# Moving half of a late adaLN into the first stage, and splitting the GDN preparation into a key and a query part

## The chip, the core and the metric

The kernel runs on one core of one Trainium2 chip. TensorE (PE) multiplies matrices, VectorE (DVE), ScalarE (ACT) and GpSimd (POOL) do the element-wise work, and SyncE (SP) and ScalarE issue the DMAs. The metric is the device time of one execution in microseconds; a time is the median of several runs.

## The reference

One layer of a hybrid diffusion backbone over 1024 latent tokens and 256 context tokens, 1024 features wide, float32. Cut to what matters here:

```python
sh1, sc1, g1, sh2, sc2, g2 = split(silu(c) @ ada_w + ada_b, 6)      # adaLN
h = modulate(rms_norm([ctx; x]), sh1, sc1)                          # context has its own sh, sc
p = h @ w_in                                                        # q k v | z | a b | rq rk rv rg
q, k, v = silu(short_conv(...))                                     # 5 taps along the tokens, per segment
# gated delta rule (GDN), chunks of 64, forward and backward:
A = strict_lower(kb @ k.T * decay); u, w = solve(I + A, [v*beta, kb*exp(G)])
# scan over chunks with qk = q @ k.T * decay; retention scan over rq, rk, rv
x = x + g1 * (concat(o_gdn, o_ret) @ w_out)
x = x + g2 * swiglu(modulate(rms_norm(x), sh2, sc2))
out = rms_norm(x)
```

The first two of the six adaLN vectors (sh1, sc1) are needed at once, the other four (g1, sh2, sc2, g2; the "late adaLN") only after the scans.

## The kernel before, in words

Tokens are cut into ten tiles of 128 (two of context, 0 and 1, and eight latent, 2 to 9). Float32 products are made of three matmuls of split operands: `split` (L343) has ScalarE copy a high part (`whi`, `hhi`) and VectorE or GpSimd subtract it to get the low part (`wlo`, `hlo`).

The program is staged as follows. Names are those that the profile prints.

1. First stage. `normalize` (L317) and `modulate` (L306) make the normalized, modulated and turned tokens `hhi`/`hlo`, in four groups of tiles (`XGROUPS`: [2,3], [4,5], [6,7,8,9], [0,1]). Token groups 0 and 1, projections with tokens as rows (matmuls `tm`, L371 to L373; 24 matmuls per tile and group of 256 columns), run while the next group is normalized.
2. `ada_rest(c, half)` (L488), the late adaLN: eight units. A unit loads 2 MB of weights in four DMAs on SP (tile `adaw2`, two buffers), adds them up on VectorE in eight operations (`acc`, L497 and L499), sums over partitions on TensorE (`gr`) and stores a row or adds a bias (L505, L512). Before, units (2,0) and (2,1) stand behind the first stage, (3,0), (3,1), (4,0), (4,1) in the loop over the k convolutions, and (5,0), (5,1) in the loop over the q convolutions.
3. Token groups 2 to 5, the small decay quantities (L563 to L598), then the k convolutions: `conv_block` (L601) of heads 4 to 7. A block is three column blocks (256 of context, 512, 512) of 24 matmuls, copied by ScalarE into `u` and, scaled, into `y` (L614, L615); VectorE adds the other four taps to `y` (L621), and ScalarE applies silu (L624). `kstat` (L634) transposes k (`kt`), makes norms and stores. A store of y goes to DRAM.
4. The q convolutions (heads 0 to 3, without context), then token groups 6 and 7 (the retention gate: ScalarE's Silu from `tm` into `res`, L532; stored as `rd`).
5. `solve(0)` and `solve(1)`. Tiles are in three batches: BATCH = [[0,1,2,9],[3,8,4,7],[5,6]]. For every tile of the batch `pre(t)` (L700) loads keys `kc` and queries `qc`, multiplies k with k (`kk`), transposes q (`qt`) for its norms (ScalarE squares, L712), and multiplies k with q (`kq`). For each of two directions it loads a broadcast row `gw`, has GpSimd select its triangle (`e`, L722), ScalarE take its exponential (L726; the table of Exp), and VectorE multiply it with `kk` (`ut`, L730, stored as `un`) and with `kq` (`sp`, L732); ScalarE and GpSimd make the other half of `sp` (L735, L736), stored in `sd`. `invert(b)` (L743) then reads `un` back (`yr`) and inverts triangular blocks on VectorE in 31 steps of two operations (`tmp` L765, `X` L767).
6. The v convolutions (heads 8 to 11), each followed by transposes on TensorE (`vT`, L856), scaled copies on ScalarE (`vt`, L859) and a store. Then `pre` of the third batch, the `merge` of the inverses (`m`), `invert(2)`, token groups 8 and 9 (z), and the scans, output projection and FFN.

The order of each engine's instructions is fixed when the kernel is built: the framework simulates a timeline and picks, among what is ready, what comes first in the program. Every engine then executes its list strictly in that order. So the v convolutions are interleaved with token groups and with `pre` and `invert`, though the program has them one after the other. PSUM banks for short products (`kk`, `qt`, `kq`, `gr`, `kt`) come from one group (`bank_b`), those of `tm` and of convolutions from two others. A pool's tiles are taken over by a later pool only when all uses are over; the memory for a stage is that of a pool opened and closed around it: `W2` and `R2` live from the first stage to the end of token group 7, then `GU`, `GI` and `GP`.

Of the kernel before, what the change touches and what calls it, by code (L numbers as in the profile page):

```python
# [38 lines left out]
def build(nc, tc, ap, dbg=None, stop=None, marks=None):  # L39
# [151 lines left out]
    try:  # L191
# [264 lines left out]
        for t in (6, 7, 8, 9, 0, 1):  # L456
            load_x(t)
        hold = None
# [3 lines left out]
        for gi, grp in enumerate(XGROUPS):  # L462
# [14 lines left out]
            if gi + 2 < len(XGROUPS):  # L477
                normalize(gi + 2, hold)
        close(P0)
# [3 lines left out]
        R2 = pool("r2", bufs=2)  # L483
        ada2 = C.tile([P, 2, KT], F32, tag="ada2", name="ada2")
        grow = [dr.tile([1, D], F32, tag="grow%d" % i, name="grow%d" % i) for i in range(2)]

        def ada_rest(c, half):

            c0 = c * D + half * 512
            src = ap["ada2"][2 * (c - 2) + half]  # L490
            acc = R2.tile([P, 512], F32, tag="acc", name="acc", bufs=1)
            for k in range(KT):
                if k % 2 == 0:
                    w = R2.tile([P, 2, 512], F32, tag="adaw2", name="adaw2", bufs=2)
                    SY.dma_start(w, src[k // 2])
                if k == 0:
                    V.tensor_scalar(acc, w[:, 0], csl[:, k, 0:1], None, ALU.mult)  # L497
                else:
                    V.scalar_tensor_tensor(acc, w[:, k % 2], csl[:, k, 0:1], acc, ALU.mult, ALU.add)  # L499
            ps = bank_b("gr")  # L500
            if c in (2, 5):
                row = R2.tile([1, 512], F32, tag="row", name="row", bufs=1)
                SY.dma_start(row, ap["adarow"][c0:c0 + 512].unsqueeze(0))
                T.matmul(ps[:1, :], ones[:, 0:1], acc, start=True, stop=True)
                V.tensor_tensor(row, row, ps[:1, :], ALU.add)  # L505
                SY.dma_start(grow[0 if c == 2 else 1][:, half * 512:(half + 1) * 512], row)
            else:
                for k in range(4):
                    T.matmul(ps[:, 2 * k:2 * k + 2], acc[:, k * P:(k + 1) * P], ones[:, 0:2], start=True, stop=True)
                ks = slice(half * 4, half * 4 + 4)  # L510
                o = ada2[:, c - 3, ks]
                V.tensor_tensor(o, ps[:, 0:8].rearrange("p (k t) -> p k t", t=2)[:, :, 0],  # L512
                                adab[:, 8 * c + 4 * half:8 * c + 4 * half + 4], ALU.add)
                if c == 4:
                    V.scalar_tensor_tensor(o, o, 1.0, gffn[:, ks], ALU.add, ALU.mult)

        nA = R2.tile([P, 8], F32, tag="nA", name="nA", bufs=1)

# [16 lines left out]
        for g in range(2):  # L535
            ada_rest(2, g)
        checkpoint("rv")

# [26 lines left out]
        V.tensor_scalar(av3[:, 1], xa[:, :, 8:16], -1.0, None, ALU.mult)  # L565
        S.activation(nA, small["alog"], AF.Exp)
# [9 lines left out]
        S.activation(be, xa[:, :, 8:16], AF.Exp, scale=-1.0)  # L576
        V.tensor_scalar(sm["beta"], sm["beta"], 1.0, None, ALU.add)
# [99 lines left out]
        for h in range(H):  # L677
            y = newy()
# [976 lines left out]
```

## Time and profile before

| | us |
|---|---|
| median of 3 runs | 1481.49 |
| the runs' range | 1479.01 to 1481.59 |
| the profiled execution | 1477.96 |
| its span | 1476.2 |
| TensorE busy | 1397.2 |
| VectorE busy | 964.6 |
| ScalarE busy | 614.0 |
| GpSimd busy | 590.3 |

The profile is of one execution. Its span is from the first to the last instruction; 1.8 us of the execution's time lie around it. An operation is named by its line and by "output<-inputs"; "xN" counts instructions. A float32 product on 128 columns counts as two matmuls in the trace where the program's order has one. A row "A <- B: total, times, longest" says that A's engine stood idle for that time until B was done. Times are in us from the start of the span, single durations in us in timelines and in ns in groups.

### The profile page before, as it was taken

The numbers are of one execution on the slowest core, as the hardware profiler recorded it, in microseconds if no ns is written. First come the engines' busy times: TensorE is split into PE (matmuls) and PEld (weight loads), VectorE is DVE, ScalarE is ACT, GpSimd is POOL, SyncE is SP. The second block draws the span as 40 slices with busy tenths as digits, with TensorE's granted clock in tenths as the row PEclk, the third lists the DMA queues.
The fourth block names the chain that finished last, engine by engine and source line by source line (L and its number), as shares of the span: only waits on it lengthen the run. The fifth ranks groups of instructions, "written<-read, shape, count | busy, mean of one in ns | idle before, by whom it ended". The sixth has DMA issues, their size and how long they took to land.

```text
span 1476.2 us, 24111 instructions
## 1 busy us (share of the span) xinstructions
PE 1397.2 (95%) x8919; PEld 1199.2 (81%) x8919; DVE 964.6 (65%) x1856; ACT 614.0 (42%) x1326; POOL 590.3 (40%) x501
## 2 busy tenths in 40 slices
PE   7999999986789999899799899999999999999997
PEld 2898888975689999898688688877888888788885
DVE  6566789289792435689676877556555564657477
ACT  5643564587333111245443623233333332444445
POOL 0120010243202344234144688898555552335321
PEclk9999999998899999999899999999999999999999
DMA  9536686688888625996532265674222242776863
GB/s 337 197 105 205 189 249 200 219 264 277 282 216 277 238 76 178 416 341 209 184 125 104 97 238 210 242 264 162 105 97 105 107 151 79 260 260 194 288 216 114
DMA packets 170421, 298.14 MB, mean 202 GB/s; under 512 B 43496, under 2 KB 93880, under 8 KB 165952
## 3 DMA queue, kind: packets, MB, share of 16 engines
q1 hardware_dynamic: 118752, 253.17, 50.2%
q10 hardware_dynamic: 49072, 35.83, 7.8%
q0 software_dynamic: 2480, 7.60, 1.4%
q8 instruction: 70, 1.15, 0.3%
q14 instruction: 47, 0.39, 0.1%
HBM read 206.60 MB, written 89.96 MB: 201 GB/s over the span
## 4 chain that ended last, share of the span: by engine, by line
PE 55%; POOL 6%; DMA 5%; DVE 4%; issue 2%; ACT 2%; SPq 1%; ACTq 0%; POOLq 0%; DVEq 0%
PE ffn L1344 7%; PE ffn L1342 6%; PE ffn L1343 6%; PE fo L1470 4%; PE fo L1469 4%; PE fo L1468 4%; PE tm L371 3%; PE tm L373 3%; PE tm L372 3%; PE op L1203 2%; PE op L1201 2%; PE op L1202 2%; DMA wd<-tw 2%; POOL ws L1315 1%; DMA pk<-sd 1%
## 5 line engine op out<-in xcount | busy, mean ns | idle before, releaser
L371 PE MATMUL tm<-whi,hhi 128*128 128x256 f32 (+1 forms) x704 | 199.5, 287 | 7.7 <-ACT vt L859 3.4
L372 PE MATMUL tm<-wlo,hhi 128*128 128x256 f32 (+1 forms) x704 | 199.3, 285 | 2.4 <-issue 2.0
L373 PE MATMUL tm<-whi,hlo 128*128 128x256 f32 (+1 forms) x704 | 197.7, 285 | 0.0
L371 PEld LDWEIGHTS tm<-whi,hhi 128*128 128x128 f32 x704 | 132.8, 190 | 11.8 <-ACT vt L859 3.6
L1342 PE MATMUL ffn<-t,whi 128*128 128x512 f32 x352 | 136.9, 390 | 1.3 <-ACT whi L344 1.3
L1344 PE MATMUL ffn<-t,wlo 128*128 128x512 f32 x352 | 137.0, 390 | 1.0 <-DVE wlo L345 1.0
L1343 PE MATMUL ffn<-t,whi 128*128 128x512 f32 x352 | 137.0, 389 | 0.0
L372 PEld LDWEIGHTS tm<-wlo,hhi 128*128 128x128 f32 x704 | 133.7, 190 | 2.1 <-issue 0.9
L373 PEld LDWEIGHTS tm<-whi,hlo 128*128 128x128 f32 x704 | 132.8, 190 | 2.6 <-issue 1.8
L344 ACT ACTIVATE whi<-wraw 128x512 fp32r<-128x512 f32 (+2 forms) x98 | 75.1, 771 | 141.4 <-PE ffn L1343 80.5
L344 ACT ACTIVATE whi<-ws 128x512 fp32r<-128x512 f32 x88 | 55.6, 632 | 171.5 <-PE ffn L1343 123.4
L345 DVE TENSOR_TENSOR wlo<-ws,whi 128x512 fp32r<-128x512 f32 x88 | 93.9, 1068 | 47.0 <-ACT whi L344 46.8
L1469 PE MATMUL fo<-wlo,ahi 128*128 128x512 f32 x308 | 120.2, 390 | 2.1 <-DVE wlo L345 2.1
L1468 PE MATMUL fo<-whi,ahi 128*128 128x512 f32 x308 | 119.3, 390 | 0.7 <-ACT ahi L344 0.7
L1470 PE MATMUL fo<-whi,alo 128*128 128x512 f32 x308 | 119.0, 390 | 0.0
L345 DVE TENSOR_TENSOR wlo<-wraw,whi 128x512 fp32r<-128x512 f32 (+2 forms) x92 | 99.4, 1082 | 24.6 <-ACT whi L344 24.6
L1342 PE MATMUL ffn<-b,whi 128*128 128x512 f32 x264 | 103.8, 393 | 4.4 <-ACT whi L344 4.4
L1344 PE MATMUL ffn<-b,wlo 128*128 128x512 f32 x264 | 103.6, 393 | 0.8 <-DVE wlo L345 0.8
L1343 PE MATMUL ffn<-b,whi 128*128 128x512 f32 x264 | 103.4, 392 | 0.0
L612 PE MATMUL b<-hlo,whi 128*128 128x512 f32 (+1 forms) x256 | 94.4, 369 | 0.0
L613 PE MATMUL b<-hhi,wlo 128*128 128x512 f32 (+1 forms) x256 | 94.3, 368 | 0.0
L611 PE MATMUL b<-hhi,whi 128*128 128x512 f32 (+1 forms) x256 | 94.3, 368 | 0.0
(446 smaller groups left out, 3448.1 us busy)
## 6 DMA issues: line engine op xcount, KB each, us to landing
adaw<-ada SPq DMA_DIRECT2D x48, 512.0 KB, 4.4
pk<-sd SPq DMA_DIRECT2D x16, 1536.0 KB, 10.0
wraw<-wfi SPq DMA_DIRECT2D x44, 512.0 KB, 3.7
ar<-ad SPq DMA_DIRECT2D x33, 512.0 KB, 4.7
w<-wfo SPq DMA_DIRECT2D x22, 512.0 KB, 5.7
wd<-tw SPq DMA_DIRECT2D x11, 1024.0 KB, 4.8
ad<-act SPq DMA_DIRECT2D x20, 512.0 KB, 3.0
raw<-wd SPq DMA_DIRECT2D x20, 512.0 KB, 4.9
```

Of the source, the lines that this page charges most:

```text
L344: S.activation(hi, raw, AF.Copy)
L345: e.tensor_tensor(lo, raw, hi.bitcast(F32), ALU.subtract)
L371: T.matmul(o, hhi[:, k, tsl], whi[:, k % 4, :], start=(k == 0), stop=False)
L372: T.matmul(o, hhi[:, k, tsl], wlo[:, k % 4, :], start=False, stop=False)
L373: T.matmul(o, hlo[:, k, tsl], whi[:, k % 4, :], start=False, stop=(k == KT - 1))
L612: T.matmul(o, whi[:, k, :], hl, start=False, stop=False)
L1342: T.matmul(o, whi[:, k, :], xhi(xn, slice(0, 4), k), start=(first and k == 0), stop=False, **kw)
L1343: T.matmul(o, whi[:, k, :], xlo(xn, slice(0, 4), k), start=False, stop=False, **kw)
L1344: T.matmul(o, wlo[:, k, :], xhi(xn, slice(0, 4), k), start=False, stop=(k == 3), **kw)
L1468: T.matmul(po[g][i], ahi[:, ts], whi, start=(j == 0 and not kw), stop=False, **kw)
L1469: T.matmul(po[g][i], ahi[:, ts], wlo, start=False, stop=False, **kw)
L1470: T.matmul(po[g][i], alo[:, ts], whi, start=False, stop=(j == FH - 1), **kw)
```

## The change

- `ada_rest` is defined earlier and takes a pool, tags and a number of buffers. Units (2,0), (2,1), (3,0), (3,1) come one each behind the four groups of the first stage, with memory from a new pool `R3`. Units (4,0), (4,1), (5,0), (5,1) come in the loop over the q convolutions, with memory from `GP`, under tags that `pre` uses as well. The loop over the k convolutions has none any more.
- `W2` is closed before the small decay quantities and `R2` opened after them and closed behind the k convolutions; `GU`, `GI` and `GP` open there. Token groups 6 and 7 take their weights from `W`, loaded on ScalarE's queue instead of SP's.
- `pre` has a key part (`kk`, `ut`, the store of `un`) and a query part (`qt`, `kq`, `sp`, the store in `sd`). The key part of batch 0 and `invert(0)` come straight behind the k convolutions. Behind them come the q convolutions, token group 6, the query part of batch 0's tiles 2 and 9, all of `pre` for batch 1 with `invert(1)`, token group 7, and the v convolutions. For tiles 2 and 9 the loads of `kc` and `gw`, GpSimd's select and the exponentials are done twice.

The core of the diff (the body of `ada_rest` is as before but for its memory, and is left out):

```diff
+        R3 = pool("r3", bufs=2)
+        xa = R3.tile([P, TT, 16], F32, tag="xa", name="xa", bufs=1)
         W2 = pool("w2", bufs=2)
-        xa = W2.tile([P, TT, 16], F32, tag="xa", name="xa", bufs=1)
...
             if gi + 2 < len(XGROUPS):
                 normalize(gi + 2, hold)
+            ada_rest(2 + gi // 2, gi % 2, R3)
         close(P0)
...
-        def ada_rest(c, half):
+        def ada_rest(c, half, pl, wtag="adaw2", atag="acc", n=1):
...
-        for g in range(2):
-            ada_rest(2, g)
         checkpoint("rv")
+        close(W2)
...
             conv_block(4 + h, y, False)
-            ada_rest(3 + h // 2, h % 2)
...
-        for h in range(H):
-            y = newy()
-            conv_block(h, y, True)
-            if h < 2:
-                ada_rest(5, h)
-            S.dma_start(qd[:, :, h, :].rearrange("t p j -> p t j"),
-                        y[:, NCTX:].rearrange("p (t j) -> p t j", j=P))
-
-        checkpoint("q")
-        for g in (6, 7):
-            token_major(g, LAT, fin_gate, S, W2, SY)
-        checkpoint("rg")
         close(R2)
-        close(W2)
...
-        def pre(t):
+        def pre(t, keys=True, queries=True):
...
+                if keys:
+                    ut = GU.tile([P, H, P], F32, tag="ut", name="ut", bufs=2)
+                    V.tensor_tensor(ut.rearrange("p h i -> p (h i)"), pk, e.rearrange("p h i -> p (h i)"), ALU.mult)
+                    SY.dma_start(un[b][:, 1 - d, c * H:(c + 1) * H, :], ut)
+                if queries:
                     sp = GP.tile([P, 2, H, P], F32, tag="sp", name="sp", bufs=2)
...
-        solve(0)
-        solve(1)
+        for t in BATCH[0]:
+            pre(t, queries=False)
+        invert(0)
+        checkpoint("inv0")
+        for h in range(H):
+            y = newy()
+            conv_block(h, y, True)
+            ada_rest(4 + h // 2, h % 2, GP, "sp", "qc", 2)
+            S.dma_start(qd[:, :, h, :].rearrange("t p j -> p t j"),
+                        y[:, NCTX:].rearrange("p (t j) -> p t j", j=P))
+        checkpoint("q")
+        token_major(6, LAT, fin_gate, S, W)
+        for t in BATCH[0]:
+            if t >= 2:
+                pre(t, keys=False)
+        for t in BATCH[1]:
+            pre(t)
+        invert(1)
+        checkpoint("inv1")
+        token_major(7, LAT, fin_gate, S, W)
         for h in range(H):
             y = newy()
             conv_block(8 + h, y, False)
```

How the order of the instructions changes, at three places. First VectorE in the first stage, where group 2 of the tokens is normalized (`rx2x`, `rx2y`, `rx2u` are steps of its reciprocal root, `xt` the tokens). Before:

```order
L128 TENSOR_SCALAR rx2x<-ms 128x4
L133 RECIPROCAL rx2y<-rx2s 128x4
L137 SCALAR_TENSOR_TENSOR rx2u<-rx2y,rx2x 128x4
L138 TENSOR_TENSOR rx2u<-rx2u,rx2y 128x4
L139 SCALAR_TENSOR_TENSOR rx2y<-rx2u,rx2y 128x4
L328 TENSOR_SCALAR xt<-xt,rx2y 128x1024 x4
```

In the changed kernel (lines from L447 on carry other numbers there):

```order
L128 TENSOR_SCALAR rx2x<-ms 128x4
L480 TENSOR_TENSOR row<-row,gr 1x512
L472 TENSOR_SCALAR acc<-adaw_857,csl 128x512
L133 RECIPROCAL rx2y<-rx2s 128x4
L474 SCALAR_TENSOR_TENSOR acc<-adaw_857,csl,acc 128x512
L137 SCALAR_TENSOR_TENSOR rx2u<-rx2y,rx2x 128x4
L474 SCALAR_TENSOR_TENSOR acc<-adaw_861,csl,acc 128x512
L138 TENSOR_TENSOR rx2u<-rx2u,rx2y 128x4
L474 SCALAR_TENSOR_TENSOR acc<-adaw_861,csl,acc 128x512
L139 SCALAR_TENSOR_TENSOR rx2y<-rx2u,rx2y 128x4
L328 TENSOR_SCALAR xt<-xt,rx2y 128x1024 x4
```

One unit's row addition and four of the next unit's operations now stand within the chain.

Second ScalarE while token group 7 is evaluated (`res`, L532, Silu; `e`, the exponentials of `pre`). Before:

```order
L532 ACTIVATE res<-tm 128x256
L387 DMA rd<-res 128x256
L726 ACT_TABLE_LOAD
L726 ACTIVATE e<-e,nG 128x128 x8
L532 ACT_TABLE_LOAD
L532 ACTIVATE res<-tm 128x256
L387 DMA rd<-res 128x256
L532 ACTIVATE res<-tm 128x256
```

In the changed kernel (L702 squares `qt`, L716 is the exponential, L724 that of `gw`):

```order
L532 ACT_TABLE_LOAD
L532 ACTIVATE res<-tm 128x256 x2
L387 DMA rd<-res 128x256 x2
L702 ACTIVATE qt,nq<-qt 128x128 x4
L716 ACT_TABLE_LOAD
L716 ACTIVATE e<-e,nG 128x128 x4
L724 ACTIVATE gw<-gw 128x512
L532 ACT_TABLE_LOAD
L532 ACTIVATE res<-tm 128x256
L387 DMA rd<-res 128x256
L716 ACT_TABLE_LOAD
L716 ACTIVATE e<-e,nG 128x128 x4
```

The pieces alternate, each with a table load; in all ScalarE's order has 28 loads in place of 20.

Third VectorE at the end of the v convolutions, with the last four long taps (`y<-u,cw,y`) of the last head. Before:

```order
L621 SCALAR_TENSOR_TENSOR y<-u,cw,y 128x1023
L765 TENSOR_TENSOR tmp<-L,X 128x231
L621 SCALAR_TENSOR_TENSOR y<-u,cw,y 128x1023
L767 TENSOR_TENSOR X<-X,tmp 128x11x21
L730 TENSOR_TENSOR ut<-kk,e 128x512
L621 SCALAR_TENSOR_TENSOR y<-u,cw,y 128x1022
L765 TENSOR_TENSOR tmp<-L,X 128x220
```

In the changed kernel:

```order
L623 SCALAR_TENSOR_TENSOR y<-u,cw,y 128x1022
L756 TENSOR_TENSOR X<-X,tmp 128x15x17
L723 TENSOR_TENSOR sp<-kq,e 128x512 x2
L623 SCALAR_TENSOR_TENSOR y<-u,cw,y 128x1023
L754 TENSOR_TENSOR tmp<-L,X 128x252
L623 SCALAR_TENSOR_TENSOR y<-u,cw,y 128x1023
L756 TENSOR_TENSOR X<-X,tmp 128x14x18
L623 SCALAR_TENSOR_TENSOR y<-u,cw,y 128x1022
```

The inversion steps around the taps are batch 0's before and batch 1's now. Batch 0's stands between token groups 6 and 7 in the new order, and two kk, qt, kq sets (tiles) that followed the last convolution on TensorE have become one.

More of the change, by code (lines that the diff above doesn't have):

```diff
@@ L478, in build @@
                 normalize(gi + 2, hold)
+            ada_rest(2 + gi // 2, gi % 2, R3)
         close(P0)
         checkpoint("h")
-        R2 = pool("r2", bufs=2)
-        ada2 = C.tile([P, 2, KT], F32, tag="ada2", name="ada2")
-        grow = [dr.tile([1, D], F32, tag="grow%d" % i, name="grow%d" % i) for i in range(2)]
-        def ada_rest(c, half):
[L489 to L517, printed above, removed]
         def fin_rope(t, o, res):
@@ L565, in build @@
         V.tensor_scalar(av3[:, 1], xa[:, :, 8:16], -1.0, None, ALU.mult)
+        nA = AB.tile([P, 8], F32, tag="nA", name="nA")
         S.activation(nA, small["alog"], AF.Exp)
```

53 lines of the change are left out of this document (37 added, 16 removed).

## The prediction

> **What bounds the kernel now.** I read first the page's busy shares, then TensorE's waits, then busy time in 20-us stretches around the moved work, and last the timelines of the widest gaps. From the page:
>
> ```profile
> PE 1397.2 (95%) x8919; PEld 1199.2 (81%) x8919; DVE 964.6 (65%) x1856; ACT 614.0 (42%) x1326; POOL 590.3 (40%) x501
> ```
>
> TensorE is the bound: 1397.2 of 1476.2 us, so 79 us of idle is all that a new order can win, and only what lies where the change acts. The change repeats no matmul, so TensorE's work stays. The stretches (start:end, length, busy time and count of PE, weight loads, DVE, ACT, POOL, then granted clock, DMA share, GB/s):
>
> ```profile
> 60.00:80.00 20.00, 17.85 (x140) 16.56 (x139) 12.72 (x22) 12.24 (x25) 5.34 (x4) 1.00 0.25 79
> 80.00:100.00 20.00, 19.70 (x163) 19.48 (x163) 9.58 (x24) 11.08 (x28) 4.46 (x5) 1.00 0.25 81
> 140.00:160.00 20.00, 20.00 (x107) 17.04 (x106) 13.40 (x20) 5.30 (x8) 0.00 (x0) 1.00 0.46 147
> 300.00:320.00 20.00, 18.17 (x109) 15.12 (x108) 13.87 (x19) 17.96 (x49) 8.30 (x7) 1.00 0.95 285
> 320.00:340.00 20.00, 16.46 (x103) 14.03 (x102) 19.66 (x35) 16.86 (x46) 8.90 (x9) 1.00 0.79 255
> 340.00:360.00 20.00, 15.07 (x85) 12.74 (x83) 19.83 (x26) 17.55 (x46) 9.83 (x8) 0.95 0.84 255
> 360.00:380.00 20.00, 8.94 (x49) 8.56 (x50) 17.57 (x33) 12.22 (x42) 6.53 (x5) 0.62 0.84 284
> 380.00:400.00 20.00, 16.62 (x141) 16.41 (x140) 13.81 (x36) 4.01 (x10) 3.49 (x4) 1.00 0.92 311
> 400.00:420.00 20.00, 15.65 (x404) 14.72 (x403) 18.47 (x48) 8.03 (x13) 0.00 (x0) 0.91 0.88 201
> 420.00:440.00 20.00, 18.79 (x488) 17.83 (x488) 18.55 (x49) 3.91 (x8) 0.95 (x1) 1.00 0.86 206
> ```
>
> PE lacks 2.45 us from 60 to 100, nothing in the k convolutions, and 21.4 us from 300 to 380 (1.83, 3.54, 4.93, 11.06), the v convolutions. There VectorE is nearly full (19.66, 19.83) and ScalarE close behind. TensorE's waits there name the ends:
>
> ```profile
> PE vT L856 <- ACT y L624: 9.6, 2, 9.3
> PE kk L705 <- issue: 8.4, 3, 6.7
> PE tm L371 <- ACT vt L859: 3.4, 1, 3.4
> ```
>
> and its timeline behind the last convolution (start, length; idle before in brackets):
>
> ```profile
> 351.22 0.39 PE L613 MATMUL b<-hhi,wlo 128*128 128x512 f32 x1
> ...
> 361.79 2.05 PE L705 MATMUL kk<-kc 128*128 128x128 f32 x8 [6.72 <-issue]
> ...
> 364.55 1.24 PE L715 MATMUL kq<-qc,kc 128*128 128x128 f32 x8
> 375.06 2.39 PE L856 MATMUL vT<-ident,y 128*128 128x128 f32 x10 [9.27 <-ACT y L624]
> ```
>
> Convolutions end at 351.6 and the last transposes (vT) at 377.45, with 6.72 + 9.27 = 16.0 us of idle. What runs between runs at a low granted clock (0.62 in that stretch): a tile's kk, qt and kq take 361.79 to 365.79, 4.0 us. VectorE in that time, in which the four taps of the last head stand apart:
>
> ```profile
> 361.62 1.27 DVE L621 SCALAR_TENSOR_TENSOR y<-u,cw,y 128x1022 f32<-128x1022 f32 x1
> ...
> 363.12 1.28 DVE L732 TENSOR_TENSOR sp<-kq,e 128x512 f32<-128x512 f32 x2
> ...
> 369.74 0.69 DVE L730 TENSOR_TENSOR ut<-kk,e 128x512 f32<-128x512 f32 x1 [1.95 <-ACT e L726]
> 370.34 1.27 DVE L621 SCALAR_TENSOR_TENSOR y<-u,cw,y 128x1022 f32<-128x1022 f32 x1
> ```
>
> The taps (1.27 each, 1.20 apart) could take 5 us and are spread from 361.62 to 371.6, by inversion steps, by ut and sp products of two tiles, and by a 1.95 us wait for an exponential. So this gap is a chain convolution, ScalarE copies, VectorE taps, silu, transposes, in competition with `pre` and `invert`.
>
> **The change part by part.** The profiled execution took 1477.96 us, 3.5 below the median of 1481.49; I sum against its own time and add 3.5 at the end. Prices on ScalarE, 300 to 380 us (busy, mean ns):
>
> ```profile
> L726 ACT ACTIVATE e<-e,nG 128x128 f32<-128x128 f32 x51 | 16.5, 393 | 6.0 <-POOL e L722 5.9
> L735 ACT ACTIVATE gw<-gw 128x512 f32<-128x512 f32 x13 | 8.0, 617 | 0.0
> L712 ACT ACTIVATE qt<-qt 128x128 f32<-128x128 f32 x24 | 6.6, 274 | 0.9 <-ACT qt L712 0.8
> L624 ACT ACT_TABLE_LOAD x4 | 5.1, 1283 | 0.1
> L624 ACT ACTIVATE y<-y 128x1280 f32<-128x1280 f32 x4 | 5.1, 1272 | 1.3 <-DVE y L621 1.2
> L615 ACT ACTIVATE y<-b,cw 128x512 f32<-128x512 f32 (+1 forms) x8 | 5.1, 635 | 0.0
> L712 ACT ACTIVATION_READ_ACCUMULATOR qt<-qt 128x1 f32 x24 | 4.8, 198 | 0.0
> L614 ACT ACTIVATE u<-b 128x512 f32<-128x512 f32 (+1 forms) x8 | 4.3, 534 | 0.0
> L344 ACT ACTIVATE whi<-wraw 128x1024 fp32r<-128x1024 f32 x3 | 3.2, 1068 | 0.0
> ```
>
> and of the late adaLN, the result copies of a token group, and a token group's matmuls at full clock (all from the views of one tile or the timeline):
>
> ```profile
> L499 DVE SCALAR_TENSOR_TENSOR acc<-adaw,csl,acc x56: 648/747/757, 99.9 to 257.6; 128x512 f32<-128x512 f32 x56
> L497 DVE TENSOR_SCALAR acc<-adaw,csl x8: 468/476/2415, 99.4 to 240.8; 128x512 f32<-128x512 f32 x8
> L532 ACT ACTIVATE res<-tm x16: 363/384/483, 125.4 to 277.0; 128x256 f32<-128x256 f32 x16
> 383.12 0.28 PE L371 MATMUL tm<-whi,hhi 128*128 128x256 f32 x1
> 383.24 0.28 PE L372 MATMUL tm<-wlo,hhi 128*128 128x256 f32 x1
> ```
>
> *AdaLN in stage 1.* A unit is 0.48 + 7 x 0.747 = 5.7 us of VectorE; four come into 60 to some 115 us, where VectorE had 7.3 and 10.4 us free in two stretches. Sums fit, but places matter: in the new order one copy and three additions stand inside the normalization chain of group 2 (0.48 + 3 x 0.747 = 2.7 us), three additions in that of group 3 (2.2). Ends: 0 and 4.9. PE is idle there for 2.45 us already; half of that can cover the same time, so I take **+3.7**. The 16 weight loads, issued on SP, meet a DMA share of 0.25. The `gr` matmuls come with them and go from later: nothing.
>
> *K convolutions.* Before, token group 6 was filler between them; now two units (2 x 5.7 = 11.4 us) precede or cut the first head's taps, and nothing but convolutions stands between. PE comes to the first `kt` after six blocks: 24 matmuls 0.23 apart are 5.6 us, half for the context block, so 28 us plus 1.4 us of the seventh. The head itself needs 14 (its blocks), 1.2 (copies), 7 (four taps of 1.2, four context ones near 0.5) and 1.3 (silu): 23.5, which leaves 5.9 us of cover for 11.4 + 1.2 (a weight split). Ends 0 (all done while the blocks run) and 6.7; **+4**, as some eight of the sixteen stand behind the context taps.
>
> *Queries and token group 7.* In the new order `res` copies (Silu) alternate with Exp. From the copy of its second token to that of its last ScalarE has 10 table loads (12.8), 24 exponentials (9.4), 6 `gw` (3.7), 16 qt squares (7.6), 7 copies (2.7) and one weight split (1.1): 37.3 us. PE has seven tokens of 24 matmuls 0.12 apart (20.3) and four tiles' kk, qt, kq, at most 2.0 each (8.0): 28.3. ScalarE is 9 us over; two tokens in flight cover 5.2 to 5.8. So 3.8 us of new idle, plus 0.7 for `gr` in the q convolutions. In the v convolutions VectorE stays almost as full, because batch 1's inversion takes batch 0's place: 3.0 us, against 5.4 before 340. Together 7.5 against 5.4: **+2.1**. The doubled work (16 exponentials, 6.3 us; four selects) is in that sum or on POOL, which is under half busy.
>
> The Trainium skill ("ScalarE: Activation LUTs", What ACT_TABLE_LOAD costs) prices a switch at 1283 ns and a drain of about 1380. The load agrees with the row to the nanosecond; the drain I do not see in the timeline, where the next activation follows the load at once:
>
> ```profile
> 271.01 1.28 ACT L532 ACT_TABLE_LOAD   x1
> 272.30 0.38 ACT L532 ACTIVATE res<-tm 128x256 f32<-128x256 f32 x1
> ```
>
> By the page the ten switches would be an estimated 13.8 us more than my sum has.
>
> *The end of the v convolutions.* One tile is left there instead of two. Chain: copies 1.2, four taps 4.8, between them what the new order puts there (two sp products 1.3, two X steps 0.4 and 1.4, one tmp 0.85), silu 1.3 without a table load: 11.2 us. PE has 2.0 for the tile and 1.1 for a transpose group in it: 8.1 idle, and 1.3 for a slow clock on the last vT (half of 2.39). Before: 16.0 idle and 3.1 (half of 4.0 and of 2.39). **-9.7**; ends -14.7, with nothing between the taps and no slow clock, and -4.
>
> The Trainium skill ("TensorE: Matmul & The Clock Gate", HAM oscillation) says that a TensorE gap above some 3.4 us brings the half clock. The 6.72 and 9.27 us gaps agree; behind the 3.38 us wait at 384 the granted clock stayed 1.00. By that rule the 4 us wait that I expect at the first `kt` brings another slow stretch, an estimated 1.5 us (half of 3.1), and 1479.7 in all; by the 3.38 us row it brings none, and my sum has none.
>
> *Behind it.* From 380 to 440 PE lacks 3.38 + 4.35 + 1.21 = 8.9 us, beside two inversions on VectorE and a DMA share near 0.9. One inversion is over by then. I take **-3.4**, ends 0 and -6.
>
> Sum: 3.7 + 4 + 2.1 - 9.7 - 3.4 = -3.3, so 1474.7 for such an execution, **1478.2** as a median.
>
> **The rivals.** *Faster, 1466.7:* the added work hides everywhere. Stage 1 (3.7), the first `kt` (4) and ScalarE's surplus (3.8) cost nothing, so -14.8. For it: VectorE free for 17.7 of 40 us from 60 to 100 and 6.6 from 140 to 160; PE fully busy in the k convolutions with taps as late. Against: the order is fixed when the kernel is built, and one late addition holds those behind.
>
> *Slower, 1486.0:* ScalarE becomes the bound in token group 7. Each `res` copy now stands behind exponentials that wait for POOL's select, and that for a load:
>
> ```profile
> POOL e L722: 28.1, 10
> ACT e L726: 11.7, 9
> ```
>
> 11.7 us in nine waits is 1.3 each; six groups of exponentials add 7.8 us, for which no cover is left: -3.3 + 7.8 = +4.5. It decides from the first group of exponentials that comes later than the `res` copy behind it, since the cover (28.3 + 5.8 = 34 us) is used up at 37.3. For it: ScalarE was 17 to 18 of 20 us busy from 300 to 360. Against: selects may come early, as POOL does little else in the token groups. With the page's drains it would be an estimated 1499.8.
>
> **How the numbers follow.** A measurement here tells 0.2%, 3 us, from nothing. Forecast 0.38, its own range 1473.5 to 1483.5; hidden everywhere 0.27; ScalarE 0.35. Faster: 0.27 and 0.18 of the forecast case, 0.45. Same: its other 0.20 and 0.03 of ScalarE's, 0.23. Slower: the other 0.32 of ScalarE's. The range reaches just past both rivals, 1465 to 1491, the upper side farther since the stage-1 and `kt` ends (1.2 and 2.7) come on top.
>
> **What would show it.** Right: PE idle near 8 us between the last convolution and the last vT, which ends about where it did (377) or 1 to 3 us earlier; PE idle 60 to 118 up by 3 to 4; a wait of the first `kt` for y of about 4; ScalarE without idle time in group 7. Wrong: vT ending before 367 (hidden everywhere), or waits of tm for `res` of 8 us and more (ScalarE).

## The result, and the profile after

| | before | after |
|---|---|---|
| median, us (runs) | 1480.37 (4) | 1512.83 (4) |
| range | 1479.01 to 1481.59 | 1509.48 to 1513.52 |
| profiled execution | 1477.96 | 1513.52 |
| its span | 1476.2 | 1511.3 |

The changed kernel is slower: the ratio is 1.022, 95% interval 1.0207 to 1.0234, some 32 us. The forecast was 1478.2 with a range to 1491, so both its sign and its range were wrong. The page's first part of the changed kernel:

```profile
PE 1413.6 (94%) x8919; PEld 1210.4 (80%) x8919; DVE 972.6 (64%) x1856; ACT 631.5 (42%) x1350; POOL 593.9 (39%) x505
```

The number of matmuls is the same (8919), yet TensorE is "busy" for 16 us more: matmuls that run at half clock take nearly twice as long (`b` matmuls start 0.23 us apart at full clock and 0.43 in the slow stretch from 136.71). So the loss has two parts, idle time and slow clock, and both are read from stretches. I cut both executions at the same five events on TensorE: the last turned token of the first stage (`xtr`), the last `kt`, the last convolution, the last `vT`, and the last merge (`m`). Between these, each row has length, busy time and count of PE, weight loads, DVE, ACT and POOL, then granted clock, DMA share and GB/s. The kernel before:

```profile
0.00:95.88 95.88, 84.68 (x517) 59.16 (x518) 56.58 (x114) 54.58 (x102) 16.50 (x19) 1.00 0.61 221
95.88:222.65 126.77, 126.77 (x768) 111.24 (x768) 94.45 (x156) 61.88 (x179) 10.41 (x5) 1.00 0.66 207
222.65:351.61 128.96, 123.59 (x759) 107.13 (x759) 95.56 (x159) 84.75 (x220) 37.46 (x35) 1.00 0.76 241
351.61:377.45 25.84, 9.85 (x62) 9.16 (x61) 23.49 (x38) 19.71 (x58) 8.69 (x7) 0.69 0.79 251
377.45:473.52 96.07, 84.90 (x1627) 81.04 (x1626) 63.98 (x165) 27.64 (x55) 11.50 (x17) 0.98 0.87 248
```

The changed kernel:

```profile
0.00:107.62 107.62, 91.39 (x536) 62.29 (x537) 75.51 (x141) 54.97 (x103) 15.82 (x19) 0.97 0.69 246
107.62:208.04 100.42, 94.71 (x527) 81.57 (x526) 66.13 (x116) 46.86 (x144) 9.64 (x6) 0.97 0.55 172
208.04:386.64 178.60, 163.93 (x1002) 143.01 (x1002) 135.93 (x240) 125.08 (x306) 48.81 (x47) 0.97 0.74 231
386.64:404.03 17.39, 5.93 (x41) 5.50 (x41) 16.91 (x29) 11.82 (x31) 2.33 (x3) 0.77 0.68 204
404.03:506.87 102.84, 86.56 (x1594) 82.25 (x1592) 40.55 (x102) 26.61 (x54) 6.67 (x9) 0.91 0.71 200
```

Lengths can't be compared, as token group 6 has moved from the second to the third stretch. What can be compared is the loss: length less PE's busy time, plus half of the busy time that falls in stretches of half clock (from the trace's list of grants). In us:

| up to | before: idle + slow | after: idle + slow | more | forecast |
|---|---|---|---|---|
| last turn | 11.2 + 0 | 16.2 + 2.8 | +7.8 | +3.7 |
| last kt | 0 + 0 | 5.7 + 3.1 | +8.8 | +4 |
| last convolution | 5.4 + 0 | 14.7 + 5.1 | +14.4 | +2.1 |
| last vT | 16.0 + 2.7 | 11.5 + 1.2 | -6.0 | -9.7 |
| last merge | 11.2 + 2.2 | 16.3 + 8.0 | +10.9 | -3.4 |
| sum | 48.6 | 84.6 | +35.9 | -3.3 |

The whole span grew by 35.1, so everything is lost by the last merge; the scans and the FFN give nothing and take nothing. Of the 35.9, 20.6 are idle and 15.3 slow clock. Single executions differ by some us in the first stretch (a run with the same order there, n1 below, lost 16.2 and not 11.2), so no row is better than that. Of its +7.8, 3.4 lie ahead of 50 us (8.3 before, 11.7 after), while the first operation of a unit starts at 57.7. Behind 50 us the loss is 2.9 before and 7.3 after. In the profiles of all kernels here it is 2.9 to 6.4 where the program has no unit in the first stage (ten kernels, mean 3.6) and 6.1 to 12.8 where it has (eight, mean 8.2): some 4 to 5 us.

The waits of TensorE in the changed kernel, to be read against the three rows of before:

```profile
PE vT L856 <- ACT y L626: 11.5, 2, 9.2
PE tm L371 <- ACT res L532: 8.3, 3, 6.5
PE b L613 <- ACT y L617: 6.6, 4, 2.5
...
PE gr L479 <- DVE acc L474: 2.6, 1, 2.6
PE xtr L334 <- DVE xt L328: 2.5, 1, 2.5
PE gr L484 <- DVE ut L719: 2.4, 1, 2.4
```

The 6.7 us wait of `kk` is gone, the 9.3 us wait of the last `vT` is 9.2 now, and a row of short ones is new: `xtr` in the first stage, `gr`, convolutions that wait for their bank (`b` behind the copy `y`), and `tm` behind `res`, 6.5 of its 8.3 us behind the v convolutions. The end of the v convolutions itself, on PE's timeline:

```profile
386.25 0.39 PE L615 MATMUL b<-hhi,wlo 128*128 128x512 f32 x1
...
390.18 1.31 PE L856 MATMUL vT<-ident,y 128*128 128x128 f32 x10 [2.22 <-ACT y L626]
...
401.64 2.40 PE L856 MATMUL vT<-ident,y 128*128 128x128 f32 x10 [9.25 <-ACT y L626]
```

From the last convolution to the last vT it is 17.4 us, against 25.8 before: the one place that got faster, as was forecast, by less (idle 11.5, forecast 8.1). It begins 35 us later.

### The profile page after: what moved, and what is told of

Read it like the earlier page. It is cut to its first block, busy times and chain, and to the rows that moved or that the text cites. A ratio compares the mean times of both kernels' runs of the same rounds, so it can differ in the third digit from the quotient of the medians.

```text
span 1511.3 us, 24154 instructions
## 1 busy us (share of the span) xinstructions
PE 1413.6 (94%) x8919; PEld 1210.4 (80%) x8919; DVE 972.6 (64%) x1856; ACT 631.5 (42%) x1350; POOL 593.9 (39%) x505
## 4 chain that ended last, share of the span: by engine, by line
PE 53%; DMA 9%; DVE 8%; POOL 6%; issue 4%; ACT 3%; SPq 1%; ACTq 0%; POOLq 0%; DVEq 0%
PE ffn L1344 7%; PE ffn L1342 7%; PE ffn L1343 7%; PE fo L1468 4%; PE fo L1470 4%; PE fo L1469 4%; PE tm L372 3%; PE tm L371 3%; PE tm L373 3%; DVE y L623 2%; PE op L1201 2%; PE op L1202 2%; PE op L1203 2%; DMA wd<-tw 2%; DVE wlo L345 1%
## 5 line engine op out<-in xcount | busy, mean ns | idle before, releaser
L371 PE MATMUL tm<-whi,hhi 128*128 128x256 f32 (+1 forms) x704 | 203.0, 292 | 14.6 <-ACT res L532 8.3
L613 PE MATMUL b<-hhi,whi 128*128 128x512 f32 (+1 forms) x256 | 97.6, 381 | 6.6 <-ACT y L617 6.6
## 6 DMA issues: line engine op xcount, KB each, us to landing
pk<-sd SPq DMA_DIRECT2D x16, 1536.0 KB, 10.4
```

Of the source, the lines that this page charges most:

```text
L371: T.matmul(o, hhi[:, k, tsl], whi[:, k % 4, :], start=(k == 0), stop=False)
L613: T.matmul(o, whi[:, k, :], hh, start=(k == 0), stop=False)
```

## The experiments

Theory A: the places of the late adaLN's units cost. Theory B: the split costs, by its order and by the weight buffers that token groups 6 and 7 lost. Theory C: the order before was a lucky one, and any other is slower. All ratios are to the kernel before on the same chip, with the 95% interval; 1% is 14.8 us.

### One half of the change at a time

**e1_ada_only.** The kernel before, with the units where the change puts them:

```diff
                 normalize(gi + 2, hold)
+            ada_rest(2 + gi // 2, gi % 2, R3)
...
-        for g in range(2):
-            ada_rest(2, g)
...
-            ada_rest(3 + h // 2, h % 2)
...
-            if h < 2:
-                ada_rest(5, h)
+            ada_rest(4 + h // 2, h % 2, R3)
```

> Only the placing of the late adaLN is changed (four units in the first stage, four in the q convolutions); GDN preparation, token groups 6 and 7 and their weights stay as before. Theory A (the adaLN units sit where they hold up TensorE: 7.8 us more idle and slow clock up to the end of the first stage, 8.4 us for the waits of gr and the slow stretch behind them in the q convolutions): slower than before by about 16 us, 1.1%. Theory B (the loss is from the split and from token groups 6 and 7 taking their weights from the convolutions' buffers): within 5 us of before.

Measured 1503.6, ratio 1.0154 (1.0133 to 1.0174), 23 us: A's side, and 7 us more than A asked. With GDN preparation as before, the new places alone cost two thirds of the loss.

**e2_split_only.** The changed kernel with the units back:

```diff
-            ada_rest(2 + gi // 2, gi % 2, R3)
...
+        for g in range(2):
+            ada_rest(2, g, R3)
...
             conv_block(4 + h, y, False)
+            ada_rest(3 + h // 2, h % 2, R2)
...
-            ada_rest(4 + h // 2, h % 2, GP, "sp", "qc", 2)
+            if h < 2:
+                ada_rest(5, h, GP, "sp", "qc", 2)
```

> All of the change but the placing of the late adaLN, whose units stand behind the first stage, in the k and in the q convolutions as before. Theory A: about half of the loss is gone, 16 us slower than before. Theory B: 25 us slower or more, with the losses in the k convolutions (8.8 us), between q and v convolutions and behind the v convolutions (10.9 us) as in the changed kernel.

Measured 1522.1, ratio 1.0293 (1.0262 to 1.0323), 43 us: B's side, and worse than the whole change. So the halves don't add up (23 + 43 against 32); they interact. TensorE's waits in the k convolutions of this run show how:

```profile
PE gr L484 <- DVE acc L474: 6.2, 1, 6.2
PE gr L479 <- DVE acc L474: 4.0, 1, 4.0
```

The units stand where they stood before. In the kernel before TensorE had no idle time in this stretch; now it stands still for their `gr`, and token group 6 is no longer there to be done meanwhile (129 `tm` matmuls in this stretch, against 286 before).

**e3_ada_k.** The changed kernel with the units of the q convolutions in the k convolutions:

```diff
             conv_block(4 + h, y, False)
+            ada_rest(4 + h // 2, h % 2, R2)
...
-            ada_rest(4 + h // 2, h % 2, GP, "sp", "qc", 2)
```

> The changed kernel, with the four adaLN units of the q convolutions moved into the k convolutions. Theory A: about 8 us faster than the changed kernel (24 us slower than before), since the two waits of gr and the slow stretch behind them go. Theory B: within 3 us of the changed kernel, because the k convolutions have no other work to fill their waits and pay for the units instead.

Measured 1517.5, ratio 1.0263 (1.0246 to 1.028), 6 us slower than the changed kernel. Neither theory's number; for what it is worth, moving four units back to the stage that hosted them did not help.

### Token group 6 and its weight buffers

**e4_before_w.** The kernel before, but for one line:

```diff
-            token_major(g, LAT, fin_gate, S, W2, SY)
+            token_major(g, LAT, fin_gate, S, W)
```

> The kernel before, with one thing changed: token groups 6 and 7 take their weights from the convolutions' buffers, loaded on ScalarE's queue, as in the changed kernel. Theory B: token group 6 can no longer be pulled forward between the k convolutions, so 9 us slower than before. Theory A: within 3 us of before.

Measured 1492.0, ratio 1.0085 (1.0063 to 1.0108), 12.6 us. The edit changes no arithmetic; it takes away the own buffers into which the weights of groups 6 and 7 were loaded early. PE's waits in the k convolutions, which were none before:

```profile
PE gr L504 <- DVE acc L499: 3.5, 1, 3.5
PE b L611 <- ACT y L615: 1.6, 1, 1.6
```

That is B's mechanism. In the profile 7.9 us are lost in the k convolutions, near B's price, then up to the last convolution 15.8 against 5.4 before, and up to the last vT 13.4 against 18.7. So this one line makes +7.9, +10.4 and -5.3 in the three middle rows of the table above, +13.0 in all, as much as the run time grew; the whole change makes +17.2 there.

**e5_tm6_k.** The changed kernel, with group 6 and buffers of its own up to the end of the k convolutions:

```diff
+        W3 = pool("w3", bufs=2)
         R2 = pool("r2", bufs=2)
...
+        token_major(6, LAT, fin_gate, S, W3, SY)
         close(R2)
+        close(W3)
...
-        token_major(6, LAT, fin_gate, S, W)
```

> The changed kernel, with token group 6 placed behind the k convolutions in the program and given weight buffers of its own (loaded on SP's queue) until the k convolutions end, so that it can fill their waits as before. Theory B (the change takes the filler away, as its memory went to the early pools): the 8.8 us of idle and slow clock in the k convolutions go, so 9 us or more faster than the changed kernel. Theory A (the places of the adaLN units): within 3 us of the changed kernel, as gr, first stage and v convolutions are what they were.

Measured 1514.8, ratio 1.0233 (1.02 to 1.0265): not faster. The second stretch (up to the last kt) and the third of this run say why:

```profile
107.91:215.68 107.77, 106.20 (x686) 96.24 (x685) 58.33 (x102) 50.48 (x152) 9.32 (x5) 1.00 0.42 124
215.68:384.57 168.89, 147.07 (x832) 125.80 (x830) 124.25 (x219) 99.43 (x252) 48.98 (x37) 0.94 0.74 235
```

In the k convolutions idle time fell from 5.7 to 1.6 us and the clock is full, just as B said; up to the last convolution it rose from 14.7 to 21.8. Group 6's matmuls can fill one stage or the other. What they fill early is missing later, when `qt` waits 6.4 us for queries that are still being loaded, and `tm` 7.5 for split weights.

**e6_split_tm6.** The same edit on e2_split_only:

```diff
+        W3 = pool("w3", bufs=2)
         R2 = pool("r2", bufs=2)
...
+        token_major(6, LAT, fin_gate, S, W3, SY)
         close(R2)
+        close(W3)
...
-        token_major(6, LAT, fin_gate, S, W)
```

> As the kernel with the split alone (adaLN units behind the first stage, in the k and the q convolutions), but with token group 6 and its own weight buffers behind the k convolutions. Theory B: idle and slow clock up to the last kt fall by 15 us or more against the split alone (33.5 there, 11.2 in the kernel before), and the time by at least as much, to 1507 or less. Theory A alone would have the split's loss elsewhere, so 1515 or more.

Measured 1511.4, ratio 1.0215 (1.0189 to 1.0241). 11 us faster than e2, but not to 1507. The loss up to the last kt was 32.4 us, as in e2 (33.5); the gain came behind the v convolutions. TensorE's waits in the k convolutions of this run:

```profile
PE tm L371 <- ACT whi L344: 5.0, 1, 5.0
PE gr L479 <- DVE acc L474: 3.6, 1, 3.6
```

The waits for `gr` fell from 10.2 us to 4.0, as the filler theory says. But the filler now has a wait of its own, 5.0 us for its weights: its first matmul starts at 141 us and its first result comes at 172, against 125 in the kernel before. So the edit did not give back what the kernel before had, and the theory in its simple form (give it back, and the k convolutions are free) is not shown.

### Steps without a reason

**n1_before_5late** and **n2_after_54** move units without a purpose:

```diff
-            if h < 2:
-                ada_rest(5, h)
+            if h >= 2:
+                ada_rest(5, h - 2)
```

> The kernel before, with the last two adaLN units in the loop over the q convolutions at heads 2 and 3 instead of 0 and 1: a step without a reason, to see how much any other order costs. Theory C (the order before was the lucky one of many, and each other order costs some 10 us by new waits and slow clock): slower by 5 us or more. Theories A and B: within 3 us of before.

```diff
-            ada_rest(4 + h // 2, h % 2, GP, "sp", "qc", 2)
+            ada_rest(5 - h // 2, h % 2, GP, "sp", "qc", 2)
```

> The changed kernel, with units (5,0) and (5,1) at the first two q heads and (4,0) and (4,1) at the last two: again a step without a reason. Theory C: off by 5 us or more to either side. Theories A and B: within 3 us of the changed kernel.

n1: 1480.1, ratio 0.9999 (0.9986 to 1.0011). n2: 1506.4, ratio 1.0164 (1.0123 to 1.0205), 6 us under the changed kernel. In the kernel before this step costs nothing; in the changed one it moves some us, as theory C has it. One step is little, but nothing here shows theory C to be the cause of 32 us. And differences of 6 us between variants of the changed kernel, as e3's, should not be read as an effect of their edit.

### Leaving the adaLN out

**e7_after_noada** and **e8_before_noada** leave out all eight units, from the changed kernel and from the kernel before. e7:

```diff
+        V.memset(ada2, 0.0)
+        for x, c in zip(grow, (2, 5)):
+            SY.dma_start(x, ap["adarow"][c * D:(c + 1) * D].unsqueeze(0))
...
-            ada_rest(2 + gi // 2, gi % 2, R3)
...
-            ada_rest(4 + h // 2, h % 2, GP, "sp", "qc", 2)
```

and e8, with the same three lines added:

```diff
-        for g in range(2):
-            ada_rest(2, g)
...
-            ada_rest(3 + h // 2, h % 2)
...
-            if h < 2:
-                ada_rest(5, h)
```

> The changed kernel without the late adaLN: its eight units are left out, a row of biases and zeros stand in their place, so the output is not the reference's. If the places of the adaLN units are the cause (theory A), this and the kernel before without them lie within 5 us of each other, near 1473 (eight gr groups of 0.8 to 1 us less than before). If the split, the order and the weight buffers that it needs are the cause (theory B), this stays 20 us or more above the other.

> The kernel before without the late adaLN, in the same way. Both theories: 1468 to 1475, since TensorE waits for no unit there and only its gr matmuls go, some 7 us.

e7: 1486.2, ratio 1.0042 (1.0024 to 1.0059). e8: 1473.2, ratio 0.9946 (0.9927 to 0.9965). This takes the loss apart. Before, the late adaLN costs 7 us (1480 to 1473), about what its `gr` matmuls take. In the changed kernel it costs 26 (1512 to 1486). So the units cost some 20 us more in the changed kernel, and the split without them 13, neither of them nothing; that the two add up to 32 follows from how they are taken. The 20 us are not the price of the places alone: with the units at their old places in the split kernel (e2) they cost 36 (1522 to 1486). Once the split has taken their filler, the new places are the better ones, by 10 us. Theory A's expectation that the two meet was wrong, and so was B's that they stay 20 apart.

**e10_after_no_stage1** and **e11_after_no_q** leave out one place each. e10:

```diff
+        V.memset(ada2[:, 0], 0.0)
+        SY.dma_start(grow[0], ap["adarow"][2 * D:3 * D].unsqueeze(0))
...
-            ada_rest(2 + gi // 2, gi % 2, R3)
```

and e11:

```diff
+        V.memset(ada2[:, 1], 0.0)
+        SY.dma_start(grow[1], ap["adarow"][5 * D:6 * D].unsqueeze(0))
...
-            ada_rest(4 + h // 2, h % 2, GP, "sp", "qc", 2)
```

> The changed kernel without the four adaLN units of the first stage, which are left out (the four in the q convolutions stay); the output is not the reference's. All eight cost 26 us there (1512 against 1486), 3 to 4 of them per four units being the gr matmuls themselves. If the first stage is the place that costs: 1488 to 1493, since only the four gr of the q convolutions remain. If the q convolutions: 1500 or more.

> The changed kernel without the four adaLN units of the q convolutions, which are left out (the four of the first stage stay); the output is not the reference's. If the first stage is the place that costs: 1502 to 1510. If the q convolutions: 1488 to 1494.

e10: 1500.2, ratio 1.014 (1.0118 to 1.0162). e11: 1500.4, ratio 1.0141 (1.0116 to 1.0166). Had one place been the cause, the run without it would have come to 1488 to 1494, and neither did. Neither place is the one: each four units cost 14 us over e7, of which 3 to 4 are matmuls.

For the first stage the mechanism is the one that was forecast. VectorE, group 2 (`rx2x` to `xt`), in the kernel before:

```profile
65.01 0.17 DVE L128 TENSOR_SCALAR rx2x<-ms 128x4 f32<-128x4 f32 x1 [3.97 <-ACT junk L325]
66.17 0.18 DVE L133 RECIPROCAL rx2y<-rx2s 128x4 f32<-128x4 f32 x1 [0.98 <-ACT rx2s L126]
...
66.97 2.74 DVE L328 TENSOR_SCALAR xt<-xt,rx2y 128x1024 f32<-128x1024 f32 x4
```

and in the changed kernel:

```profile
68.56 0.17 DVE L128 TENSOR_SCALAR rx2x<-ms 128x4 f32<-128x4 f32 x1
69.73 0.67 DVE L480 TENSOR_TENSOR row<-row,gr 1x512 f32<-1x512 f32 x1 [1.00 <-PE gr L479]
70.33 0.47 DVE L472 TENSOR_SCALAR acc<-adaw,csl 128x512 f32<-128x512 f32 x1
...
72.76 0.75 DVE L474 SCALAR_TENSOR_TENSOR acc<-adaw,csl,acc 128x512 f32<-128x512 f32 x1 [1.09 <-DMA adaw<-ada]
...
74.41 2.74 DVE L328 TENSOR_SCALAR xt<-xt,rx2y 128x1024 f32<-128x1024 f32 x4
```

From `rx2x` to `xt` it takes 5.9 us, against 2.0 before. The 2.7 us of unit operations were in the sum; the row addition (0.67 us), and that an operation in the chain brings its own wait, 1.09 us for a weight load, were not. The wait of 1.00 us for `gr` adds nothing: before, the chain stood 0.98 us at this place for `rx2s`. That `rx2x` comes 3.6 us later is not the units' doing: group 1's `xt` is 3.4 us late already (52.2 against 48.8), ahead of the first unit.

For the units of the q convolutions, the place in the program is not the place in the order: the scheduler pulled (4,0) and (4,1) up into the small decay quantities ahead of the k convolutions. VectorE in e10, where no unit of the first stage disturbs the picture (`L476` and `L474` are a unit's operations, `L155` to `L574` the chain that ends in `g`), and what TensorE waited for:

```profile
115.61 0.49 DVE L474 TENSOR_SCALAR acc<-adaw,csl 128x512 f32<-128x512 f32 x1 [1.64 <-DMA adaw<-ada]
...
120.30 0.32 DVE L155 SCALAR_TENSOR_TENSOR spa<-spa,spq 128x160 f32<-128x160 f32 x1
120.53 0.74 DVE L476 SCALAR_TENSOR_TENSOR acc<-adaw,csl,acc 128x512 f32<-128x512 f32 x1
121.20 0.32 DVE L155 SCALAR_TENSOR_TENSOR spa<-spa,spq 128x160 f32<-128x160 f32 x1
121.43 0.74 DVE L476 SCALAR_TENSOR_TENSOR acc<-adaw,csl,acc 128x512 f32<-128x512 f32 x1
...
125.42 0.23 DVE L574 TENSOR_TENSOR g<-sps,nA 128x80 f32<-128x80 f32 x1
```

```profile
PE G L585 <- DVE g L574: 5.7, 1, 5.7
```

Operations of 0.32 us alternate with additions of 0.74, one of the unit's operations waits 1.64 us for its load, and TensorE stands 5.7 us for the `g` at their end. The kernel before has the same alternation, of other units, but TensorE does token group 6 meanwhile (its first `res` comes at 125.4).

### Queues, buffers and tables

**e9_after_zg.** The changed kernel, with z's stores on GpSimd's queue:

```diff
         for g in (8, 9):
-            token_major(g, LAT, fin_gate, S, W)
+            token_major(g, LAT, fin_gate, G, W)
```

> The changed kernel, with the stores of token groups 8 and 9 issued on GpSimd's queue, not ScalarE's, for the wait of 6.5 us of tm for res behind the v convolutions and the slow stretch after it. If those stores are late because they queue behind the stores of vt on ScalarE's queue, 6 to 10 us faster than the changed kernel; if the transfers as such are late (the DMA engines' share is 0.95 there), within 3 us of it.

1511.2, ratio 1.0207 (1.0179 to 1.0234): no difference in time. Its trace shows no wait of `tm` for `res` behind the v convolutions any more, but `m` waits 5.2 us for a load and 8.4 behind an inversion step, and the loss up to the last merge is 24.0 us, as in the changed kernel (24.3). So that wait was not what bounds this stretch; moving the stores to another queue only changes which wait is seen.

**e12_before_noada_w.** e4's line, in the kernel before without adaLN (e8):

```diff
-            token_major(g, LAT, fin_gate, S, W2, SY)
+            token_major(g, LAT, fin_gate, S, W)
```

> The kernel before without the late adaLN (left out, the output is not the reference's), with token groups 6 and 7 taking their weights from the convolutions' buffers. If that sharing is what the split costs: 1486, 13 us above the kernel before without adaLN. If the costs are in the order of preparation and inversion: within 4 us of 1473.

1474.1, ratio 0.9975 (0.9954 to 0.9995), 1 us above e8 by the medians, 4 by the ratios, whose intervals overlap. So shared weight buffers cost 12 us when adaLN units have to be waited for, and little when there are none: a filler is worth what it covers. And the split's 13 us are not the buffers, but for a few us. The last two stretches of e12 and of e7 point to a place (last convolution to last vT, then to the last merge); e12:

```profile
360.28:378.92 18.64, 5.93 (x42) 5.55 (x41) 18.09 (x33) 11.14 (x28) 4.84 (x3) 0.71 0.61 220
378.92:471.96 93.04, 87.04 (x1627) 83.14 (x1626) 59.70 (x153) 27.94 (x56) 9.79 (x17) 0.95 0.84 248
```

and e7:

```profile
363.26:382.37 19.11, 7.31 (x45) 6.81 (x44) 18.66 (x31) 14.20 (x39) 5.08 (x4) 0.64 0.56 199
382.37:483.41 101.04, 87.58 (x1608) 83.00 (x1607) 40.78 (x100) 26.62 (x54) 9.73 (x14) 0.93 0.77 224
```

Behind the v convolutions e7 takes 8 us longer than e12, with 13.5 us idle on PE against 6.0. Against e8, the kernel before without units, it is 3 us (101.0 to 98.0): there the larger part of the split's loss lies up to the last convolution (20.1 against 6.4). So the place of the 13 us is not settled by single executions. In e7 VectorE has a third less to do behind the v convolutions than in e12 (40.8 against 59.7), since one inversion fewer is left, and it does not help.

**e13_noada_tm7** and **e14_after_tm7** move token group 7 in e7 and in the changed kernel:

```diff
         token_major(6, LAT, fin_gate, S, W)
+        token_major(7, LAT, fin_gate, S, W)
...
-        token_major(7, LAT, fin_gate, S, W)
```

> The changed kernel without the late adaLN (left out, the output is not the reference's), with token group 7 placed straight behind token group 6, ahead of the query parts and of batch 1. ScalarE's order then has 24 table loads, not 28. If the split's 13 us come from ScalarE's alternating table loads and the copies of res behind exponentials: near 1476, 10 us below the run without adaLN. If they come from where preparation and inversion end and the merges begin: within 4 us of 1486.

> The changed kernel with adaLN, and token group 7 straight behind token group 6 (18 table loads in ScalarE's order, not 28). ScalarE as the cause: 10 us or more faster than the changed kernel's 1512. Otherwise within 4 us of it.

e13: 1486.8, ratio 1.0049 (1.0032 to 1.0066), as e7. So half of the eight more table loads, and the copies of `res` behind exponentials, go without a gain: ScalarE's tables are not the cause of the split's 13 us. e14: 1505.5, ratio 1.018 (1.0161 to 1.0199), 6 us under the changed kernel, which neither side expected. It is as much as n2's step, and n2's order, too, has fewer table loads (22). But the stretch up to the last convolution, in which these loads stand (19 in the changed kernel, 9 in e14, 14 in n2), lost no less: 19.8, 19.8 and 22.9 us.

## Why the prediction was wrong

*AdaLN in the first stage (forecast +3.7): the mechanism was right; in the stage the size was near, by luck, and the run time paid more.* The stretch lost 7.8 us more, but 4.4 of them behind 50 us, where units act. In the run time four units there cost 14 us, about 4 of them matmuls that the prediction put at nothing, since they leave another place (they are in the 7 us of the kernel before); where the rest falls single executions do not settle. The step that failed: only the durations of four of the operations in the chain were counted, not the row addition, not the 1.09 us wait for a load, nor that 2.5 us of `xtr` waiting are followed by half clock. The chain of group 2 grew by 3.9 us, not 2.7, and more of that was covered than the sum allowed.

*K convolutions (+4): wrong; +8.8, half of which the sum had by luck, for another wait.* The first `kt` waited 0.4 us. TensorE waited for `gr`, for `GT` and for banks, ahead of the first kt, because the units cut the decay chain; the step that failed is that two units "precede or cut the first head's taps": it looked for their harm at the first `kt` (162 us), while 4.4 of the 5.7 us of idle lie between 120 and 140.

*Queries and group 7 (+2.1): wrong; +14.4.* ScalarE's sum of 37 us was not what decided: `tm` waited 1.8 us in all for `res` up to the v convolutions. Instead there are seven waits of 0.6 to 2.6 us for `gr`, weights, banks and loads, and two stretches of half clock. The step that failed is the sum of one engine's surplus: the waits are those of other chains. e4, which has the order of preparation as before and only the shared weight buffers, loses 15.8 us in this stretch, so some 10 of the 14 us come with the buffers that token groups 6 and 7 lost, a term that this sum does not have.

*End of the v convolutions (-9.7): right in kind; -6.0.* The idle time was 11.5 and not 8.1. One tile in place of two stands there, as forecast. But e4 and e12, without the split, have one tile there too, and lose 13.4 and 13.9 us against 12.7: the gain does not need the early inversion.

*Behind it (-3.4): wrong in sign; +10.9.* The step that failed was "One inversion is over by then", taken as a gain: of TensorE's waits there in the kernel before, none is put down to VectorE. The first merge comes 31.2 us after the last vT (435.2) against 26.8 (404.2), and TensorE waits 6.5 us for `res` and 5.2 inside merges. The program opens the pools of the merges' tiles (`GM`, `G2`) only behind the v convolutions, so an earlier inversion alone does not bring the first merge forward. On the chain that ended last one store of `res` takes 12.8 us, and 3.3 in the kernel before. Why is open: moving the stores off ScalarE's queue (e9) leaves the loss as it is. Nor is it the split's alone: e1, with the units moved and no split, loses 23.8 us in this stretch, as the changed kernel does (24.3; e1's profile is of its slowest execution).

*The slow clock: not in the sum, and 15 of the 36 us (within the rows above).* The prediction weighed a rule of the Trainium skill ("TensorE: Matmul & The Clock Gate", HAM oscillation: gaps above some 3.4 us bring the half clock) against the 3.38 us wait that brought none, and took no charge for new short waits. The trace differs from the rule, below.

The rivals: "hidden everywhere" was wrong. "ScalarE in token group 7" had the right sign, and by the letter its mark was met, waits of `tm` for `res` of 8 us and more (8.3). But 6.5 of them lie behind the v convolutions; up to there they are 1.8 us, and e13 speaks against it too.

What the experiments leave: 20 us that the adaLN units cost more in the changed kernel, about equal for the two places, by waits that the traces show and a filler that is gone; and 13 us for the split without units. How the 13 are caused, and where they arise, stays open. By stretches, one part of the change, the shared weight buffers with the units at their old places (e4), makes +13.0 of the +17.2 between the last turn and the last vT.

## What to carry to other kernels

A work unit that costs nothing where it is has a filler beside it; ask what TensorE does while it waits in the new place, and whether the buffers that let that filler start early are still there after the change. A step put into an in-order engine's chain costs its own waits as well as its time, and where the scheduler may move it, read the order, not the program. To share a loss among parts that interact, leave one part out of both kernels, and say that the shares hold for this way of taking apart: single halves here gave 23 and 43 us of a loss of 32.

## What the runs showed of the hardware

TensorE's half clock follows windows on a fixed grid. In the changed kernel it is granted, among others, from 75.28, 136.71 and 239.11 us on; these lie 61.4 and 102.4 us apart, 18 and 30 times 3.413, and every half-clock stretch but the one at the end of the run is a multiple of 3.41 us long. The windows ahead of and behind these starts, and two from the same grid around a gap of 2.6 us (PE's column is its busy time, the clock stands behind POOL):

```profile
71.87:75.28 3.41, 0.93 (x9) 0.73 (x8) 2.48 (x6) 0.38 (x1) 0.00 (x0) 1.00 0.90 301
75.28:78.69 3.41, 2.97 (x13) 2.05 (x13) 3.37 (x6) 0.97 (x2) 0.00 (x0) 0.50 0.50 159
133.30:136.71 3.41, 0.83 (x6) 0.48 (x5) 2.34 (x9) 0.76 (x4) 0.00 (x0) 1.00 0.58 186
136.71:140.13 3.42, 2.79 (x7) 2.21 (x8) 2.17 (x4) 1.65 (x4) 0.00 (x0) 0.50 0.68 195
235.70:239.11 3.41, 1.07 (x6) 0.63 (x5) 1.42 (x3) 2.38 (x7) 0.70 (x2) 1.00 0.79 263
239.11:242.53 3.42, 3.41 (x12) 3.13 (x13) 3.38 (x4) 1.75 (x6) 1.55 (x1) 0.50 0.87 155
273.24:276.66 3.42, 1.60 (x14) 1.40 (x12) 3.06 (x8) 1.10 (x3) 0.00 (x0) 1.00 0.42 159
276.66:280.07 3.41, 2.54 (x13) 1.48 (x14) 3.34 (x8) 0.61 (x1) 0.00 (x0) 1.00 0.09 16
```

A window with 2.3 to 2.6 us of idle, in one gap (71.87) or in several short ones (133.30), is followed by half clock. The gap of 2.6 us at 275, as long as the others, falls on two windows (1.8 and 0.9 us idle) and brings none. The 3.38 us wait at 384 in the kernel before, on which the prediction leaned, brought none either: the grid cuts it into 1.63 and 1.75. With the grid laid over the traces of all 18 kernels, each of the 192 full-clock windows with over 1.9 us of idle is followed by half clock, and none of the 6992 with under 1.0; in between both happen. So a wait of 2.4 us can cost another 1.7 (half of 3.4) or nothing, by where it falls; the 3.4 us of the Trainium skill's rule ("TensorE: Matmul & The Clock Gate", HAM oscillation) are the window's length here, not the least gap. A schedule with many waits of 1 to 3 us pays for this, and one with none doesn't.
